# First stage: later thirds' token tiles normalised and transposed during the preceding third, kept in DRAM, loaded into the operand buffers block by block

## The chip, the cores and the metric

The kernel runs on one core of one Trainium2 chip. The metric is the device time of one execution in microseconds, the median of several runs. Nothing is changed in what is computed.

## The reference

One layer of a hybrid encoder over 16 learned meta tokens and 2048 input tokens (together T = 2064), width 1024, float32:

```
p  = rms_norm(h, norm_mix_pre) @ w_in                  # 1024 -> 3080 columns
oa = rg_lru_group(p[:, :512])                          # columns "a": convolution, gates, linear recurrence
ob = forgetting_attention_group(p[:, 512:2056])        # "q", "k", "v" and 8 gate columns "f"
oc = rwkv7_group(p[:, 2056:])                          # columns "c": delta-rule recurrence over time
h  = h + rms_norm(concat(oa, ob, oc) @ w_out, norm_mix_post)
f  = causal_dwconv3(rms_norm(h, norm_ffn_pre) @ ffn_up)
h  = h + rms_norm((gelu(gate) * val) @ ffn_down, norm_ffn_post)
```

The change is within the first line: the norm of h, and the product with w_in.

## The kernel before

**Stages.** In order: the first stage (input projection, with the two recurrences beside it), attention, output projection with the second norm, FFN up, FFN down. Everything between stages goes through scratch tensors in DRAM (scr).

**The first stage.** The product is made transposed: 128 columns of w_in are the stationary operand, up to 400 tokens the moving one, and the contraction of 1024 is KD = 8 slices of 128. For precision every operand is split into a rounded part and a remainder (hi, lo: xh, xl for the tokens, wh, wl for the weights), and a product is three matmuls (mm3, lines 174 to 176; tile psp). The tokens are cut in three parts, each of two blocks (w_in_tokens, L182): 400 and 384 tokens, 384 and 384, 256 and 256. The operands of a part's two blocks stand in pool xn, which has one buffer for each of xh0, xl0, xh1, xl1.

**The norm.** w_in_norm (L189) makes a part's operands, tile by tile of 128 tokens: norm_transpose (L123) loads the tile into a buffer xt (tag nt_x), takes the sum of squares on ScalarE (L119), the inverse root in nine short steps on VectorE (L86 to L95), scales (L132), and transpose_split (L136) turns it with eight transposes on TensorE (L145, tile pst) in two groups; each group is rounded into xh by ScalarE (L151) and the remainder written to xl by VectorE (L152). Parts 1 and 2 are normalised when the part before has been issued, since only then the xn buffers come free. In part 1 all tiles but the first two are held until the last weight of part 0 has been rounded (issue_after).

**The units.** w_in_part (L304) goes through 24 units of 128 columns in the order c (8), a (4), k, v, q (4 each). A unit takes its weights once (w_in_weights, L211) and runs both blocks; the last two units run together, both on block 0 and then both on block 1. In part 0 the weights are loaded raw (nt_x), rounded (L168, L169) and written to scr wk; parts 1 and 2 load both halves from there (L222), into pool w (two buffers each of wh and wl) or, for half of part 2's units, into nt_x. Ahead of the units, w_in_gate (L275) makes the eight gate columns for both blocks, two matmuls a slice (L293, L294; tile psf), from a weight fw in pool w. Results leave PSUM by turns through ScalarE (L57, L240) and VectorE (L59, L241) into pool st, and SP stores them (L242, L243, L249, L268).

**Pools.** nt has four nt_x buffers (raw weights, xt, the splitting of w_out, some weights), st two of each tag, the PSUM pool of the stage five banks for psp, psf, pst.

**What runs beside.** recurrences (L2070) is a list of small steps: the gate's cumulative sum, and for nine blocks of 256 tokens the RWKV block (tiles named rw.., PSUM rps and eps, lines 1015 to 1359) and the LRU block (L1426 to L1468, tile rwlraw its load). Beside.advance hands out 1.25 steps after each step of a unit, from the 13th unit of part 0 on; what is left over when the units are done is issued then (L2183), and runs on into the attention. In parts 1 and 2 two more helpers are called between units: up_sums (loads us, L1681, sums on GpSimd) and, in part 1, w_out_split.

**Order.** Nearly all DMAs are issued from SP, in one in-order queue. The program issues instructions in the order told here; the build then draws up each engine's order by priority along a simulated timeline, and issue_after is an order by hand on one engine. The engines run in the order drawn up.

## Time and profile before

| | |
|---|---|
| time, median of 3 runs | 2990.34 us (2987.96 to 2994.16) |
| span of the profiled execution (the page has no other time of it) | 2994.3 us |
| first stage, from the first psp to the last | 42 to 880 us |
| PE, DVE, ACT busy over the span | 97%, 68%, 49% |
| mean granted TensorE clock | 0.976 |

In the profile PE is the matmul side of TensorE and PEld its weight load, DVE is VectorE, ACT ScalarE, POOL GpSimd, SP the engine that issues the DMAs. A row of the busy time by stretch gives for each engine its busy time and, in brackets, its instructions, then the granted clock, the busy share of the 16 DMA engines and their rate. A row of the timeline gives start, duration, engine, line, operation and tile, and in square brackets the idle time ahead of it with what ended it. Durations of matmuls include their way through the array, so successive ones overlap: their rate is read from their starts.

### The profile page before, as it was taken

What the parts mean: (1) busy time and instruction counts of PE and PEld (TensorE: products, weight loads), DVE (VectorE), ACT (ScalarE), POOL (GpSimd) and SP (SyncE); (2) the same over time, 40 slices, a digit from 0 to 9 for tenths busy, and PEclk for the clock granted to TensorE, in tenths of its full rate; (3) what the DMA queues carried; (4) which work ended last, traced back from release to release, by engine and by line L of the source; (5) the groups of instructions that cost most, each with busy time, mean ns of one, the idle gap of its engine ahead of it and who ended that gap; (6) DMA issues with size and microseconds to landing.
All of it is one profiled execution on the core that took longest, in us unless ns stands there. A gap on an engine that the chain in (4) does not pass through costs nothing.

```text
span 2994.3 us, 52802 instructions
## 1 busy us (share of the span) xinstructions
PE 2898.0 (97%) x18694; PEld 2486.3 (83%) x18694; DVE 2037.0 (68%) x3937; ACT 1480.8 (49%) x2858; POOL 1319.7 (44%) x1567
## 2 busy tenths in 40 slices
PE   6999999999999999999999999999999999999998
PEld 6998899888886655665568999999999999787887
DVE  5258644765677776565636998898778787656766
ACT  4246332443346554455634656666565665424333
POOL 1002122121223665666843667446655544656443
PEclk9999899999988999999999999999999999999999
DMA  6777469676644347544336565577777764436453
GB/s 210 239 235 226 135 230 310 203 242 194 199 129 101 95 109 208 134 113 109 77 96 212 183 198 179 173 220 211 208 208 218 222 198 128 158 116 220 145 174 120
DMA packets 469190, 530.49 MB, mean 177 GB/s; under 512 B 85710, under 2 KB 355736, under 8 KB 467372
## 3 DMA queue, kind: packets, MB, share of 16 engines
q1 hardware_dynamic: 468156, 526.17, 58.2%
q8 instruction: 147, 2.41, 0.3%
q0 software_dynamic: 768, 0.93, 0.1%
q14 instruction: 119, 0.97, 0.1%
HBM read 368.07 MB, written 158.90 MB: 176 GB/s over the span
## 4 chain that ended last, share of the span: by engine, by line
PE 59%; DVE 4%; POOL 2%; DMA 2%; ACT 2%; issue 2%; SPq 0%; DVEq 0%; POOLq 0%; ACTq 0%
PE psu L174 9%; PE psu L175 9%; PE psu L176 9%; PE po L716 4%; PE psd L174 4%; PE psd L175 4%; PE psd L176 4%; PE mx L566 2%; PE pswo L174 2%; PE pswo L176 2%; PE pswo L175 2%; PE sc L693 2%; PE sc L694 2%; POOL acc L737 1%; DVE mc L571 1%
## 5 line engine op out<-in xcount | busy, mean ns | idle before, releaser
L175 PE MATMUL psu<-xo,uw 128*128 128x344 f32 x1848 | 591.4, 320 | 0.0
L174 PE MATMUL psu<-xo,uw 128*128 128x344 f32 x1848 | 586.0, 322 | 2.7 <-ACT u L1828 1.2
L176 PE MATMUL psu<-xo,uw 128*128 128x344 f32 x1848 | 581.9, 320 | 1.3 <-POOL uw L1657 1.0
L174 PE MATMUL psp<-xh,wh 128*128 128x384 f32 (+2 forms) x1152 | 380.8, 331 | 0.0
L176 PE MATMUL psp<-xh,wl 128*128 128x384 f32 (+2 forms) x1152 | 378.0, 328 | 0.0
L175 PE MATMUL psp<-xl,wh 128*128 128x384 f32 (+2 forms) x1152 | 377.8, 328 | 0.0
L1657 DVE TENSOR_TENSOR uw<-uq,uw 128x512 fp32r<-128x512 f32 x341 | 320.3, 944 | 59.2 <-ACT uw L1656 56.7
L174 PEld LDWEIGHTS psu<-xo,uw 128*128 128x128 f32 x1848 | 345.8, 188 | 4.3 <-DVE vb L1848 1.8
L176 PEld LDWEIGHTS psu<-xo,uw 128*128 128x128 f32 x1848 | 345.7, 188 | 2.1 <-POOL uw L1657 1.3
L175 PEld LDWEIGHTS psu<-xo,uw 128*128 128x128 f32 x1848 | 347.1, 188 | 0.0
L1656 ACT ACTIVATE uw<-uq 128x512 fp32r<-128x512 f32 x462 | 287.9, 627 | 95.7 <-PE psu L176 44.4
L698 ACT ACTIVATE p<-sc,bias 128x512 f32<-128x512 f32 (+4 forms) x352 | 197.9, 590 | 142.3 <-PE sc L694 119.2
L571 DVE TENSOR_REDUCE mc<-mx 128x1 f32<-128x512 f32 (+6 forms) x352 | 190.0, 565 | 113.6 <-PE mx L566 80.1
L1796 DVE SCALAR_TENSOR_TENSOR uy<-psu,ffn_cols,uy 128x342 f32<-128x342 f32 (+1 forms) x390 | 220.4, 567 | 61.4 <-ACT uy L1794 59.7
L1804 POOL TENSOR_TENSOR uy<-uy,uy 128x342 f32<-128x342 f32 (+1 forms) x132 | 146.5, 1110 | 229.2 <-DVE uy L1796 55.9
L737 POOL TENSOR_TENSOR acc<-acc,p 128x512 f32<-128x512 f32 (+3 forms) x208 | 222.7, 1073 | 48.4 <-DVE acc L737 23.4
L1657 POOL TENSOR_TENSOR uw<-uq,uw 128x512 fp32r<-128x512 f32 x121 | 184.4, 1524 | 133.8 <-ACT uw L1656 116.0
L174 PEld LDWEIGHTS psp<-xh,wh 128*128 128x128 f32 x1152 | 220.1, 191 | 8.7 <-issue 7.3
L176 PEld LDWEIGHTS psp<-xh,wl 128*128 128x128 f32 x1152 | 220.1, 191 | 7.0 <-issue 5.1
L175 PEld LDWEIGHTS psp<-xl,wh 128*128 128x128 f32 x1152 | 220.1, 191 | 5.0 <-issue 3.2
L1657 DVE TENSOR_TENSOR fo<-u,fo 128x896 fp32r<-128x896 f32 x88 | 101.6, 1155 | 133.7 <-ACT fo L1656 133.2
L1656 ACT ACTIVATE fo<-u 128x896 fp32r<-128x896 f32 x88 | 81.2, 923 | 206.6 <-PE psd L176 118.1
(488 smaller groups left out, 6409.4 us busy)
## 6 DMA issues: line engine op xcount, KB each, us to landing
uq<-scr_us SPq DMA_DIRECT2D x220, 256.0 KB
uq<-in_ffn_up_dram SPq DMA_DIRECT2D x209, 256.0 KB
wl<-scr_wk SPq DMA_DIRECT2D x48, 512.0 KB
wh<-scr_wk SPq DMA_DIRECT2D x48, 512.0 KB
u<-scr_ff SPq DMA_DIRECT2D x88, 256.0 KB
scr_ff<-uy SPq DMA_DIRECT2D x110, 171.0 KB
raw<-in_w_in_dram SPq DMA_DIRECT2D x24, 512.0 KB
scr_wk<-wh SPq DMA_DIRECT2D x24, 512.0 KB
```

The costliest lines, as they stand in the source:

```text
L174: nc.tensor.matmul(out, ah, bh, start=first, stop=False, skip_group_check=more)
L175: nc.tensor.matmul(out, ah, bl, start=False, stop=False, skip_group_check=more)
L176: nc.tensor.matmul(out, al, bh, start=False, stop=last, skip_group_check=more)
L566: nc.tensor.matmul(ps[:rows, : e - a], q3[:, qo : qo + rows], k2[:, a:e], start=True, stop=not last)
L571: self.reduced = nc.vector.tensor_reduce(mc[:rows, i, ci : ci + 1], ps[:rows, : e - a], axis=AX.X, op=ALU.max)
L698: last = nc.scalar.activation(p[:rows, :w], ps[:rows, :w], AF.Exp, bias=bias[:rows, j : j + 1])
L716: mm = nc.tensor.matmul(po[at : at + 64, c0:n], v1[:rows, j], p[:rows, : n - c0], start=start and i < 2, stop=end and i + 2 >= len(group), ...
L737: eng.tensor_tensor(a, ps_[0][0][:rows, c0:n] if start and i == 1 else a, p[:rows, : n - c0], op=ALU.add)
L1656: core.nc.scalar.activation(hi, src, AF.Copy)
L1657: (eng or core.nc.vector).tensor_tensor(lo, src, hi, op=ALU.subtract)
L1796: core.conved = stt(y[:, :n], src[:, i : n + i], cw[:, 44 * i + cc : 44 * i + cc + 1], y[:, :n], op0=ALU.mult, op1=ALU.add)
L1804: core.pooled = nc.gpsimd.tensor_tensor(v[:, :n], g[:, :n], v[:, :n], op=ALU.mult)
```

## The change

The norm of parts 1 and 2 is taken apart. w_in_ahead makes the tiles of a later part while the part before runs: six tiles of part 1 after the units 0, 2, 4, 6, 8, 10 (counted from 0) of part 0, four tiles of part 2 after the units 2, 6, 10, 14 of part 1. Load, squares, root and scaling are as before (normed); the transposed groups are copied from PSUM once, unsplit (by turns ScalarE and VectorE), and stored to a new scratch tensor xt. At the start of part 1 and of part 2 w_in_fetch loads each block in four pieces of two slices into the buffer of the remainder, rounds each on ScalarE and takes the remainder in place on VectorE. The hold of part 1's tiles is gone. In parts 1 and 2 the gate and the first two units go block by block (gate, unit 0, unit 1 on block 0, then the same on block 1), and the gate's weights and unit 0's stand in nt_x.

```diff
--- before.py
+++ after.py
@@ -120,17 +120,21 @@
     return rstd_from(core.nc, v, ss, width, core.apart)
 
 
-def norm_transpose(core, pools, psum, src, rows, gain, pieces, after=nullcontext):
+def normed(core, pools, src, rows, gain):
 
     nc = core.nc
     xt = pools["nt"].tile([P, D], F32, tag="nt_x", name=core.n("xt"))
     nc.sync.dma_start(xt[:rows], src)
     junk = pools["st"].tile([P, D], BF16, tag="stv", name=core.n("xj"))
     v = pools["nt"].tile([P, 6], F32, tag="rs", name=core.n("rs"))
-    with after():
-        rs = rstd_of(core, v[:rows], xt[:rows], D, junk[:rows])
+    rs = rstd_of(core, v[:rows], xt[:rows], D, junk[:rows])
     nc.vector.scalar_tensor_tensor(xt[:rows], xt[:rows], rs, gain[:rows], op0=ALU.mult, op1=ALU.mult)
-    transpose_split(core, psum, xt, rows, pieces)
+    return xt
+
+
+def norm_transpose(core, pools, psum, src, rows, gain, pieces):
+
+    transpose_split(core, psum, normed(core, pools, src, rows, gain), rows, pieces)
 
 
 def transpose_split(core, psum, xt, rows, pieces):
@@ -186,7 +190,7 @@
     return [tiles[a:e] for a, e in zip(cuts, cuts[1:])]
 
 
-def w_in_norm(core, pools, psum, x, meta, gain, part):
+def w_in_blocks(core, pools, part):
     blocks = []
     for b, tl in enumerate(w_in_tokens(part)):
         t0 = tl[0][0]
@@ -194,28 +198,63 @@
         hi = pools["xn"].tile([P, KD, n], F32R, tag=f"xh{b}", name=core.n("xh"))
         lo = pools["xn"].tile([P, KD, n], F32R, tag=f"xl{b}", name=core.n("xl"))
         blocks.append((t0, n, tl, hi, lo))
+    return blocks
+
+
+def w_in_norm(core, pools, psum, x, meta, gain):
+    blocks = w_in_blocks(core, pools, 0)
     for t0, n, tl, hi, lo in blocks:
         for s, rows in tl:
             src = meta if s < META else x[s - META : s - META + rows, :]
-            late = part == 1 and (s, rows) not in blocks[0][2][:2]
-            after = (lambda: core.tc.issue_after(core.rounded.ins)) if late else nullcontext
-            norm_transpose(core, pools, psum, src, rows, gain, [(hi, lo, s - t0, 0, rows)], after)
+            norm_transpose(core, pools, psum, src, rows, gain, [(hi, lo, s - t0, 0, rows)])
     return blocks
 
 
+def w_in_ahead(core, pools, psum, x, gain, scr, part):
+
+
+    nc = core.nc
+    for b, tl in enumerate(w_in_tokens(part)):
+        for s, rows in tl:
+            xt = normed(core, pools, x[s - META : s - META + rows, :], rows, gain)
+            for k0 in range(0, KD, 4):
+                ps = psum.tile([P, 4, P], F32, tag="mm", name=core.n("pst"))
+                for k in range(4):
+                    nc.tensor.transpose(ps[:, k], xt[:, (k0 + k) * P : (k0 + k + 1) * P], core.ident[:])
+                o = pools["st"].tile([P, 4, P], F32, tag="stv", name=core.n("xs"))
+                core.evac(o[:], ps[:])
+                c = s - tl[0][0]
+                nc.sync.dma_start(scr["xt"][part - 1, b, :, k0 : k0 + 4, c : c + P], o[:])
+            yield
+
+
+def w_in_fetch(core, pools, scr, part):
+    nc = core.nc
+    blocks = w_in_blocks(core, pools, part)
+    for b, (t0, n, tl, hi, lo) in enumerate(blocks):
+        for k0 in range(0, KD, 2):
+            ks = slice(k0, k0 + 2)
+            raw = lo[:, ks].bitcast(F32)
+            nc.sync.dma_start(raw, scr["xt"][part - 1, b, :, ks, :n])
+            nc.scalar.activation(hi[:, ks], raw, AF.Copy)
+            nc.vector.tensor_tensor(lo[:, ks], raw, hi[:, ks], op=ALU.subtract)
+    return blocks
+
+
 def w_in_kept(scr, c0):
 
     return scr["wk"][c0 // P]
 
 
-def w_in_weights(core, pools, w_in, c0, scr, part):
+def w_in_weights(core, pools, w_in, c0, scr, part, first=False):
 
     if part == 0:
         src = w_in[:, c0 : c0 + P].rearrange("(k p) c -> p k c", p=P)
         pair = split_load(core, pools["w"], (pools["nt"], "nt_x", None), src, [P, KD, P], "w")
     else:
-        core.turns += part == 2
-        pl, tags = (pools["nt"], ("nt_x", "nt_x")) if core.turns % 4 > 1 else (pools["w"], ("wh", "wl"))
+        core.turns += part == 2 and not first
+        other = first or core.turns % 4 > 1
+        pl, tags = (pools["nt"], ("nt_x", "nt_x")) if other else (pools["w"], ("wh", "wl"))
         pair = [pl.tile([P, KD, P], F32R, tag=tag, name=core.n(s)) for s, tag in zip(("wh", "wl"), tags)]
     for t, kept in zip(pair, w_in_kept(scr, c0)):
         t = t[:].rearrange("p k c -> p (k c)").bitcast(F32)
@@ -276,7 +315,8 @@
 
     nc = core.nc
     c0 = 2048
-    w = pools["w"].tile([P, KD, P], F32R, tag="wh", name=core.n("fw"))
+    pl, tag = (pools["nt"], "nt_x") if part else (pools["w"], "wh")
+    w = pl.tile([P, KD, P], F32R, tag=tag, name=core.n("fw"))
     flat, kept = w[:].rearrange("p k c -> p (k c)").bitcast(F32), w_in_kept(scr, 3 * D)[0]
     if part == 0:
         raw = pools["st"].tile([P, KD, 8], F32, tag="stv", name=core.n("fraw"))
@@ -297,12 +337,11 @@
         o = pools["st"].tile([8, 400], F32, tag="stl", name=core.n("fo"))
         nc.vector.tensor_tensor(o[:, :n], ps[0:8, :n], a[:, :n], op=ALU.add)
         nc.sync.dma_start(scr["f"][:, t0 : t0 + n], o[:, :n])
-    yield False
-    yield True
+        yield
 
 
 def w_in_part(core, pools, psum, w_in, blocks, scr, part):
-    yield from w_in_gate(core, pools, psum, w_in, blocks, scr, part)
+    gate = w_in_gate(core, pools, psum, w_in, blocks, scr, part)
     units = [("c", 2056 + P * i) for i in range(8)] + [("a", P * i) for i in range(4)]
     units += [(s, c + P * i) for s, c in (("k", 1024), ("v", 1536), ("q", 512)) for i in range(4)]
     waiting = [None]
@@ -314,7 +353,20 @@
             waiting[0]()
         waiting[0] = after
 
-    for kind, c0 in units[:-2]:
+    first = 2 if part else 0
+    some = [
+        (w_in_weights(core, pools, w_in, c0, scr, part, i == 0), kind, c0) for i, (kind, c0) in enumerate(units[:first])
+    ]
+    for block in blocks:
+        next(gate)
+        yield part == 0 and block is blocks[-1]
+        for w, kind, c0 in some:
+            step(w, block, kind, c0)
+            yield block is blocks[-1]
+    if part:
+        yield True
+
+    for kind, c0 in units[first:-2]:
         w = w_in_weights(core, pools, w_in, c0, scr, part)
         for block in blocks:
             step(w, block, kind, c0)
@@ -343,6 +395,7 @@
         "part": dr.tile([SEQ, D], F32, name="scr_part"),
         "us": dr.tile([NFF, P, 4 * 512], F32, name="scr_us"),
         "wo": dr.tile([KD, 2, P, D], F32, name="scr_wo"),
+        "xt": dr.tile([2, 2, P, KD, 384], F32, name="scr_xt"),
         "wk": dr.tile([3 * D // P + 1, 2, P, D], F32, name="scr_wk"),
         "ds": dr.tile([DOWN_PAIRS, P, 4 * 512], F32, name="scr_ds"),
     }
@@ -2028,6 +2081,8 @@
 
 
 READY = 13
+
+AHEAD = range(1, 13, 2), range(4, 18, 4)
 PACE = 1.25
 
 WIDE = (0, 5)
@@ -2132,18 +2187,20 @@
             pools = {"xn": pool(p1a, "xn", 1), "nt": pool(p1a, "nt", 4), "w": pool(p1a, "w", 2), "st": pool(p1a, "st", 2)}
             sums = up_sums(core, pool(p1a, "us", 1), a["ffn_up"], scr, EARLY)
             split_out = w_out_split(core, pools["nt"], a["w_out"], scr)
-            following = w_in_norm(core, pools, ps_mm, x, meta, g_pre, 0)
+            ahead = [w_in_ahead(core, pools, ps_mm, x, g_pre, scr, part) for part in (1, 2)]
             for part in range(3):
-                blocks = following
+                blocks = w_in_fetch(core, pools, scr, part) if part else w_in_norm(core, pools, ps_mm, x, meta, g_pre)
                 if part == 0:
                     zeros = pools["st"].tile([P, PAD], F32, tag="sth", name="zeros")
                     nc.vector.memset(zeros[:], 0.0)
                     for r in range(0, A_ROWS + C_ROWS, P):
                         nc.gpsimd.dma_start(scr["p"][r : r + P, 0:PAD], zeros[:])
                 units = w_in_part(core, pools, ps_mm, a["w_in"], blocks, scr, part)
-                for _ in range(READY if part == 0 else 0):
+                for i in range(READY if part == 0 else 0):
                     while not next(units):
                         pass
+                    if i in AHEAD[0]:
+                        next(ahead[0])
                 if part == 0:
                     attn_consts(core)
                     rk = rwkv_consts(
@@ -2173,13 +2230,13 @@
                         continue
                     if part == 1 and i > 1:
                         next(split_out, None)
+                    if part == 1 and i in AHEAD[1]:
+                        next(ahead[1])
                     if part and i % 2 == 0:
                         with tc.issue_after(core.loaded.ins):
                             next(sums, None)
                     i += 1
                 run(sums) if part == 2 else None
-                if part < 2:
-                    following = w_in_norm(core, pools, ps_mm, x, meta, g_pre, part + 1)
         beside.finish()
         for _ in R.ending:
             pass
```

## The prediction

> **What bounds the kernel now.** I read the page first (engines, clock), then busy time by stretch, then the order of TensorE's work (PE) at the two places where one third of the first stage ends and the next begins.
>
> ```profile
> span 2994.3 us, 52802 instructions
> ...
> PE 2898.0 (97%) x18694; PEld 2486.3 (83%) x18694; DVE 2037.0 (68%) x3937; ACT 1480.8 (49%) x2858; POOL 1319.7 (44%) x1567
> ...
> PEclk9999899999988999999999999999999999999999
> ```
>
> PE is busy for 97% of the span, so only PE time that is wasted can be won: waits, or work at a reduced granted clock. The stretches of the first stage and the one behind it:
>
> ```profile
> core 0: us, PE busy (x) PEld busy (x) DVE busy (x) ACT busy (x) POOL busy (x), PEclk, DMA share, GB/s
> 42.00:150.00 108.00, 108.00 (x605) 108.00 (x604) 30.66 (x42) 31.93 (x44) 0.40 (x1) 1.00 0.70 230
> 150.00:279.00 129.00, 128.28 (x736) 118.04 (x736) 89.70 (x220) 65.38 (x128) 9.82 (x18) 1.00 0.73 233
> 279.00:323.00 44.00, 38.87 (x390) 32.43 (x389) 39.23 (x104) 27.34 (x54) 13.40 (x20) 0.69 0.37 114
> 323.00:617.00 294.00, 291.95 (x2420) 267.12 (x2419) 159.33 (x387) 99.53 (x187) 57.30 (x84) 0.98 0.71 232
> 617.00:627.00 10.00, 7.98 (x54) 7.11 (x53) 7.63 (x17) 6.00 (x13) 2.97 (x4) 0.86 0.94 306
> 627.00:880.00 253.00, 246.58 (x2622) 224.41 (x2622) 162.90 (x415) 108.75 (x223) 56.64 (x91) 0.97 0.62 190
> 880.00:1120.00 240.00, 221.62 (x1964) 150.37 (x1961) 182.70 (x502) 134.37 (x291) 130.80 (x205) 0.87 0.46 107
> ```
>
> Parts 0, 1 and 2 are rows 1 and 2, row 4 and row 6. Between them lie two seams of 44 and 10 us. In the first the granted clock is 0.69 and DVE is busy 39.2 of 44 us. The timeline of PE shows its edges:
>
> ```profile
> 278.74 0.34 PE L176 MATMUL psp<-xh,wl 128*128 128x384 f32 x1
> 278.91 1.80 PE L145 MATMUL pst<-ident,xt 128*128 128x128 f32 x15
> ...
> 320.21 0.34 PE L294 MATMUL psf<-xl,fw 128*128 128x384 f32 x1
> ...
> 322.68 0.34 PE L294 MATMUL psf<-xl,fw 128*128 128x384 f32 x1
> 322.86 0.34 PE L174 MATMUL psp<-xh,wh 128*128 128x384 f32 x1
> ```
>
> The products of the projection (psp) stop at 279 and resume at 323. From 320.21 to 322.68 there are 14 steps: 0.176 us per 384-wide matmul at full clock.
>
> **What the change removes at seam 1.** The other work that PE does there (recurrences rps and eps, gate psf) remains. Busy time in the two seams by tile, columns PE, PEld, DVE, ACT; first rps, then eps, then psf:
>
> ```profile
> 279.00:323.00 44.00, 17.78 (x296) 16.03 (x296) 4.89 (x9) 5.12 (x10) 0.69 0.37 114
> ```
> ```profile
> 279.00:323.00 44.00, 6.01 (x12) 2.68 (x12) 0.88 (x2) 2.71 (x6) 0.69 0.37 114
> ```
> ```profile
> 279.00:323.00 44.00, 8.09 (x32) 7.01 (x32) 0.54 (x1) 0.48 (x1) 0.69 0.37 114
> 617.00:627.00 10.00, 3.44 (x17) 3.15 (x17) 0.00 (x0) 0.21 (x1) 0.86 0.94 306
> ```
>
> At full clock rps and eps need about (17.8 + 6.0) × 0.69 = 16.4 us, psf 32 × 0.176 = 5.6: 22 of the 44 us. The other **22.0 us** go if the operands are there on time. Where part 0 has psp without a break, row 1 above, the clock is 1.00, so the recurrences should keep full clock between products.
>
> **Seam 2.** The same timeline:
>
> ```profile
> 617.25 3.62 PE L145 MATMUL pst<-ident,xt 128*128 128x128 f32 x28
> 622.88 0.66 PE L145 MATMUL pst<-ident,xt 128*128 128x128 f32 x4 [2.00 <-DVE xl L152]
> ...
> 629.26 0.28 PE L294 MATMUL psf<-xl,fw 128*128 128x256 f32 x1
> ...
> 631.06 0.28 PE L174 MATMUL psp<-xh,wh 128*128 128x256 f32 x1
> ```
>
> A 256-wide matmul takes 1.80 / 15 = 0.12 us. The 10 us hold 17 psf and 5 psp, 2.6 us at that rate; **7.4 us** go.
>
> **What comes back elsewhere.** The transposes stay PE work. A transpose takes 3.62 / 28 = 0.129 us; six tiles of eight are 48 × 0.129 = **6.2 us**, now in part 0, and four tiles are 32 × 0.129 = **4.1 us** in part 1. PE has no free time there (108.0 of 108), so both count in full. Net: seam 1 −15.8, seam 2 −3.3, together **−19.1 us**.
>
> The rest of each tile, grouped by line in seam 1 (ahead of the bar: busy us, mean ns behind it):
>
> ```profile
> L152 DVE TENSOR_TENSOR xl<-pst,xh 128x512 fp32r<-128x512 f32 x12 | 7.9, 679 | 0.3 <-ACT xh L151 0.3
> L151 ACT ACTIVATE xh<-pst 128x512 fp32r<-128x512 f32 x12 | 6.8, 612 | 0.4 <-PE pst L145 0.3
> L132 DVE SCALAR_TENSOR_TENSOR xt<-xt,rs,g_pre 128x1024 f32<-128x1024 f32 x2 | 2.5, 1272 | 0.0
> L119 ACT ACTIVATE xj<-xt 128x1024 bf16<-128x1024 f32 x2 | 2.2, 1102 | 0.2 <-DMA xt<-in_x_dram 0.2
> ```
>
> A tile made ahead costs ACT 1.1 + one evacuation 0.6, DVE 1.3 + nine short root steps + one evacuation 0.7: for six tiles some 10 us of ACT and 20 of DVE, about 12 beside the root steps. In part 0 up to 150 us DVE is busy 31 of 108 and ACT 32, so this lies beside products. It would surface if it made the weights late; they have slack:
>
> ```profile
> L168 ACT ACTIVATE wh<-raw 128x1024 fp32r<-128x1024 f32 x13 | 13.8, 1059 | 33.1 <-PE psp L175 32.0 <-DMA raw<-in_w_in_dram 1.1
> ```
>
> In 42:150 the rounding of a weight waits 32.0 us for the buffer that PE still reads and 1.1 for its transfer, so a raw buffer (nt_x, four) lent to a tile is not missed. SP's queue gets one load and two stores per tile where there was one load, and eight loads per fetch. The added traffic is ten 0.5 MB stores and as much in loads back, 10.5 MB: 45 us at row 4's 232 GB/s, in 600 us of a share near 0.7. This stretch bore more (tile psp: PE, clock, DMA share, GB/s):
>
> ```profile
> 500.00:520.00 20.00, 18.06 (x100) 1.00 0.97 353
> ```
>
> Psp held 18 of 20 us at 353 GB/s. But part 1's third and fourth tile come near there. I take **+2 us** for transfers that come late, with weights of part 2's third unit, which now wait for the gate's nt_x buffer; bounds 0 and 7 (one pair of 512 KB weights late by its whole transfer, priced below). The gate's weights and the first unit's, moved to nt_x, cost nothing: they can now load before the last products end. Gate and two units by block hold the same matmuls as before.
>
> **What the new wait costs.** A block's buffers come free with the last product that reads them. The last two units of a part run block by block, so block 0 is free 48 × 0.176 = 8.4 us ahead of the part's end. Its fetch is 1.57 MB in seam 1, 1.05 MB in seam 2. The nearest transfers, from the queue's and ACT's timelines:
>
> ```profile
> 284.70 1.15 SPq L127 DMA_DIRECT2D xt<-in_x_dram x2
> ...
> 287.60 23.57 SPq L1426 DMA_DIRECT2D rwlraw<-scr_p x3
> ```
> ```profile
> 291.77 1.06 ACT L119 ACTIVATE xj<-xt 128x1024 bf16<-128x1024 f32 x1 [0.25 <-DMA xt<-in_x_dram]
> ```
>
> Two loads, 1.05 MB, took 7 us from first issue to use; 1.57 MB then some 9 us. Splitting a piece of 128x768 is scaled from these 896-wide rows of the page:
>
> ```profile
> L1657 DVE TENSOR_TENSOR fo<-u,fo 128x896 fp32r<-128x896 f32 x88 | 101.6, 1155 | 133.7 <-ACT fo L1656 133.2
> L1656 ACT ACTIVATE fo<-u 128x896 fp32r<-128x896 f32 x88 | 81.2, 923 | 206.6 <-PE psd L176 118.1
> ```
>
> ACT 0.8, DVE 1.0 us. Behind the last piece that is 1.8 us alone, some 6 behind DVE's other work (70% busy in row 2). Block 0 is ready 11 to 15 us after its release, 2 to 7 after the part's end: I take **+5 us**, nearer the upper end since DVE is fullest there. Block 1 has the gate and two units on block 0 to hide behind (16 + 48 matmuls, 11.2 us, and the recurrences): 0. In seam 2: ready 8 to 11 us against 8.4, and block 1 against 64 × 0.12 = 7.7 us of cover: **+2**, bounds 0 and 6. While the fetch waits, SP's later stores and loads stand behind it: outputs in two-buffer st tiles, then the PSUM banks, then PE itself; that is the slow rival below.
>
> A rule on the clock: the Trainium skill, "TensorE: Matmul & The Clock Gate", Part 1, says that the clock falls to half after one idle window of about 3.4 us, and Part 4 that transposes do not count as activity. The trace agrees: 0.69 and 0.86 in the seams, where transposes and small products ran. By it my 5 us wait would leave another window at half clock, an estimate of 1.7 us more, and the sum would be −8. A rule on transfers: the Trainium skill, "DMA: Bandwidth & Descriptors", Anatomy of one DMA, gives 2.0 us + bytes / 436 GB/s (measured on GpSimd's path), an estimate of 5.6 us for 1.57 MB; the sum would then be about −13. The measured 7 us for 1.05 MB decides, and no run here shows the 436.
>
> **The sum.** −19.1 + 5 + 2 + 2 = **−10 us**. It is made against the profiled execution: the page gives its span, 2994.3, and nothing around it; that is 0.1 us over the longest of the three times and 4.0 over their median of 2990.3. Carried to the median: **2980**. The build draws up each engine's order from a simulated timeline, so orders far from the seams can shift; I allow ±8 us.
>
> **Rivals.**
> *The fetch is wholly hidden.* DVE loses about 20 us of norm work in seam 1 and gets 8 × 1.0 back, so block 0 is on time: −19 us, 2971. For it: DVE's 39 of 44. Against: DVE is 70% busy before the seam as well.
>
> *The queue holds the fetch back (slower).* SP issues in order. From 287.6 it spent 23.6 us on three issues, with waits. If block 0's loads stand behind such a wait at seam 1, PE has only recurrences at half clock, as now: −10 + 23.6 = +14, 3004. From 16 us of such waiting on it is slower by over 0.2% (about 6 us, what a measurement of this kernel can tell from no change). For it: the row. Against: that wait fell where DVE was filled by the norms, which leave.
>
> *The recurrences give it back.* They run on into the attention:
>
> ```profile
> 880.00:900.00 20.00, 18.71 (x178) 13.83 (x175) 14.72 (x39) 1.93 (x6) 8.23 (x6) 0.50 0.69 163
> ```
>
> In 880:1120 the clock is 0.87 and PE 222 of 240. In the seam they caught up by 16 us of PE work. If their chain, not PE, ends that stretch, products that end 10 us earlier lengthen it by as much: 2988 to 2990. For it: the clock of 0.50 at 880. Against: they are handed out by units, and PE's order stays theirs.
>
> **How the numbers follow.** Forecast 2980: 0.42. Hidden, 2971: 0.20. Given back, 2989: 0.14. Queue, 3004: 0.24. Faster: 0.62, same 0.14, slower 0.24. The range runs from 2963 (hidden, with the 8 us of shifted order) to 3003, which takes in all but the queue's worse half and the outermost shifts. The forecast's own range, by its bounds of 0 to 7, 0 to 6 and 0 to 7: −19 to +1, 2971 to 2991.
>
> **What would show it.** Right: no transposes of xt left between the parts; psp breaks off for some 5 us plus gate at seam 1 and 2 at seam 2; granted clock there above 0.9; part 0 longer by 6 us, part 1 by 4; DVE's share in the seam down. Wrong: gate products waiting on DVE or on the fetch for over 15 us, SP standing ahead of the fetch, psp in part 0 waiting for weights, or 880:1120 longer by what the seams lost.

## The result and the profile after

The changed kernel takes 3015.5 us (median of four executions; 3006.2 to 3018.5) where the kernel before, measured beside it, takes 2992.3: a ratio of 1.0074, 95% interval 1.0054 to 1.0094. It is slower by 0.7%; the forecast was 2980 and the range ended at 3003. Executions of one and the same kernel scatter by 5 to 29 us, the longer ones mostly with the lower mean granted clock (here 3006.2 us at 0.979, 3018.5 at 0.971). So verdicts below go by ratios of several executions, and stages, each read from one execution, are trusted where several kernels show them alike.

The page of the changed kernel:

```profile
span 3016.2 us, 52920 instructions
...
PE 2895.6 (96%) x18694; PEld 2486.8 (82%) x18694; DVE 2048.8 (68%) x3943; ACT 1491.2 (49%) x2864; POOL 1315.9 (44%) x1567
...
PEclk9999999999987899999999999999999999999999
...
DMA packets 483078, 540.98 MB, mean 179 GB/s; under 512 B 86286, under 2 KB 368600, under 8 KB 481260
```

TensorE (PE) is busy for 2.4 us less than before (2898.0) in a span that is 21.9 us longer: what was added is time in which PE does nothing. To find the place, busy time by stretch, cut at the first and the last product (psp) of each part; the last two rows are the **tail**, from the last psp until 30% of the attention's po products are done:

```profile
core 0: us, PE busy (x) PEld busy (x) DVE busy (x) ACT busy (x) POOL busy (x), PEclk, DMA share, GB/s
43.67:284.20 240.53, 240.53 (x1386) 230.27 (x1386) 132.71 (x283) 104.65 (x184) 10.27 (x19) 1.00 0.80 256
284.20:288.06 3.86, 3.86 (x27) 3.82 (x26) 3.78 (x8) 2.76 (x6) 0.00 (x0) 1.00 1.01 270
288.06:623.28 335.22, 321.77 (x2784) 292.21 (x2784) 193.40 (x482) 127.55 (x237) 66.98 (x104) 0.96 0.69 227
623.28:627.92 4.64, 4.64 (x34) 4.01 (x34) 3.56 (x6) 1.31 (x3) 0.87 (x1) 1.00 1.07 373
627.92:891.45 263.53, 254.41 (x2687) 230.20 (x2685) 163.23 (x412) 109.80 (x223) 60.95 (x97) 0.96 0.61 187
891.45:977.25 85.80, 70.15 (x599) 50.60 (x598) 63.15 (x172) 44.73 (x99) 31.43 (x52) 0.72 0.52 118
977.25:1165.76 188.51, 166.30 (x1355) 107.72 (x1355) 135.72 (x367) 98.14 (x208) 102.36 (x161) 0.91 0.43 103
```

The same cuts of before, those that the prediction does not show:

```profile
42.15:278.74 236.59, 235.87 (x1338) 225.66 (x1338) 120.11 (x261) 97.05 (x172) 10.23 (x19) 1.00 0.72 232
...
626.72:877.96 251.24, 244.82 (x2612) 222.87 (x2612) 161.62 (x413) 108.57 (x222) 56.64 (x91) 0.98 0.62 191
877.96:964.33 86.37, 78.56 (x678) 57.35 (x677) 66.44 (x192) 44.11 (x98) 34.24 (x54) 0.71 0.54 122
964.33:1147.36 183.03, 168.50 (x1381) 107.60 (x1381) 134.26 (x359) 98.68 (x210) 103.83 (x162) 0.93 0.44 104
```

Seam 1 shrank from 44.1 to 3.9 us, with PE never idle; seam 2 from 9.6 to 4.6. Against these 45 us stand part 0 (+3.9), part 1 (294.2 to 335.2, +41.0), part 2 (+12.3) and the tail (+4.9): together 17 of the 22 us, the rest in small pieces outside these cuts. The recurrence steps that the seam had held had to reappear in part 1. The question is what the rest is.

### The profile page after: what moved, and what is told of

The parts are those of the page before. It is cut to its first block, busy times and chain, and to the rows that moved or that the text cites. A ratio compares the mean times of both kernels' runs of the same rounds, so it can differ in the third digit from the quotient of the medians.

```text
span 3016.2 us, 52920 instructions
## 1 busy us (share of the span) xinstructions
PE 2895.6 (96%) x18694; PEld 2486.8 (82%) x18694; DVE 2048.8 (68%) x3943; ACT 1491.2 (49%) x2864; POOL 1315.9 (44%) x1567
## 4 chain that ended last, share of the span: by engine, by line
PE 79%; DVE 7%; DMA 5%; POOL 3%; ACT 3%; issue 2%; SPq 1%; DVEq 0%; POOLq 0%; ACTq 0%
PE psu L178 9%; PE psu L179 9%; PE psu L180 9%; PE psp L180 5%; PE psp L178 5%; PE psp L179 5%; PE psd L178 4%; PE psd L179 4%; PE psd L180 4%; PE po L769 4%; PE mx L619 2%; PE pswo L178 2%; PE pswo L179 2%; PE pswo L180 2%; PE sc L746 2%
## 5 line engine op out<-in xcount | busy, mean ns | idle before, releaser
L624 DVE TENSOR_REDUCE mc<-mx 128x1 f32<-128x512 f32 (+5 forms) x352 | 190.0, 565 | 122.2 <-PE mx L619 83.3
L178 PEld LDWEIGHTS psp<-xh,wh 128*128 128x128 f32 x1152 | 221.9, 193 | 10.2 <-issue 7.3
```

What stands on the lines that cost most here:

```text
L178: nc.tensor.matmul(out, ah, bh, start=first, stop=False, skip_group_check=more)
L624: self.reduced = nc.vector.tensor_reduce(mc[:rows, i, ci : ci + 1], ps[:rows, : e - a], axis=AX.X, op=ALU.max)
```

## The experiments

Three theories stood first: **A**, the recurrences cost more between products than in the seam; **B**, one accident of order; **C**, late transfers and tiles. After these **T** (the tiles made ahead in part 1 lose), **F** (the fetch and the weights at the start of part 2 lose) and **O** (any change draws up another order of the small steps, and that costs). The other letters (T1, T2, P, S, W) are explained in the expectation that first uses them. The **projection** is the time from the first psp to the last, seams included. In the diffs `NEW` names the parts that fetch; with `(1, 2)` it is the changed kernel, with `()` the kernel before.

**1. Without recurrences**, in the kernel before and in the changed one (one run each):

```diff
-    for b in ((0, 1, 2), (3, 4, 5), (6, 7, 8))[part]:
+    for b in ():
```

> The kernel before without the RWKV and LRU blocks beside the projection (the gate's cumulative sum stays; the rows of scr mix that they would write are zeroed). Leaves out: both recurrences. It is the base for e1_norec_after: the first stage should shrink well below 880 us, seam 1 keep its stop of products. Theory A (the recurrences used the seam, and cost more among the products) expects seam 1 here to be 44 - 24 = some 20 us, nearly all of it norm work. Theory C (the added traffic or the fetch itself costs) says nothing on this one.

> The changed kernel without the RWKV and LRU blocks (rows of scr mix zeroed). Leaves out: both recurrences. Theory A: with no recurrences to hand back, the change must gain what it takes from the seams less the transposes: the last product of part 2 comes 10 to 20 us earlier than in e1_norec_before. Theory C (traffic, fetch, weights that come late): it gains nothing or loses 10 us or more, as in the full kernel. Theory B (one wait of 7 us in part 1 and the half clock behind it, an accident of the order) expects a gain of 10 or more here too, since that wait is one of the recurrence.

Measured: 2698.3 and 2717.5 us. These are single executions, and 19 us is within what two of one kernel can differ by; the stages say more. The projection is 16.7 us longer with the change (610.1 to 626.8), though seam 1 shrinks by 22.6: it is part 1 that grows, by 32.9. Part 1 without recurrences, before and changed:

```profile
280.04:492.48 212.44, 211.13 (x1202) 208.16 (x1201) 44.73 (x101) 39.87 (x67) 34.13 (x44) 1.00 0.87 290
```
```profile
262.89:508.23 245.34, 222.44 (x1249) 219.81 (x1249) 58.77 (x112) 47.19 (x78) 39.09 (x48) 0.96 0.84 284
```

A expected a gain of 10 to 20 us with no recurrence in the program, so A falls. Much of the cost can be seen here, in the waits of PE in part 1 of the changed kernel without recurrences (waited for: us in total, times, longest):

```profile
PE pst L223 <- DVE xt L131: 18.8, 4, 10.4
```

Each of the four tiles made ahead in part 1 makes PE wait for its scaling. The fourth of them, by the timelines of the DMA queue, ACT, DVE and PE:

```profile
412.64 0.60 SPq L1557 DMA_DIRECT2D scr_wo<-wo  x1
413.30 0.48 SPq L127 DMA_DIRECT2D xt<-in_x_dram  x1
```
```profile
422.20 1.06 ACT L119 ACTIVATE xj<-xt 128x1024 bf16<-128x1024 f32 x1 [5.52 <-DMA xt<-in_x_dram]
```
```profile
425.17 1.28 DVE L131 SCALAR_TENSOR_TENSOR xt<-xt,rs,g_pre 128x1024 f32<-128x1024 f32 x1
```
```profile
426.51 1.75 PE L223 MATMUL pst<-ident,xt 128*128 128x128 f32 x7 [10.36 <-DVE xt L131]
```

The load goes out behind the transfers of w_out's pieces, which share its buffers (nt_x); it takes 8.9 us from issue to first use (the four loads took 6.4 to 8.9), where seam 1 of the kernel before had two loads in 7; the root and the scaling follow, and the transposes stand in PE's order ahead of the next unit's products, so PE waits 10.4 us. In part 0 of the full changed kernel a load at 60.4 us fed transposes at 91.0, and nothing waited; here 13 us lie between issue and transposes. B falls as the whole, with no recurrence there to meet an accident; C is nearest.

**2. One part alone**: `NEW = (1,)` and `NEW = (2,)`.

> The change at part 1 alone: six tiles ahead in part 0, fetch at the start of part 1; part 2 normalised between the parts as before, no tiles ahead in part 1. Theory A (seam 1's recurrence work comes back dearer): slower than before by 8 to 20 us. Theory B (the 7 us wait stands behind the fourth tile ahead in part 1): that wait is gone, time -5 to +5 us against before. Theory C (traffic): about half of the loss, +10 us.

> The change at part 2 alone: four tiles ahead in part 1, fetch at the start of part 2; seam 1 as before, with its held tiles. Theory A: seam 2 holds hardly any recurrence work, so -7.4 + 4.1 = -3 us, within 5 us of before. Theory B (tiles ahead in part 1 push the recurrence's short chain on VectorE behind them): slower by 8 to 15 us. Theory C: about half of the loss, +10 us.

Measured: part 1 alone 2979.8 us, ratio 0.9953 (0.9934 to 0.9973), **faster**; part 2 alone 3023.7, ratio 1.0092 (1.0059 to 1.0126), slower. None of the three theories had either time. The first half of the change gains; the loss is in the half that serves part 2. Seam 1, part 1 of the first kernel, then part 1 of the second:

```profile
282.01:285.87 3.86, 3.86 (x27) 3.82 (x26) 3.25 (x8) 3.28 (x7) 0.00 (x0) 1.00 1.00 299
285.87:600.94 315.07, 310.93 (x2736) 280.49 (x2736) 185.25 (x455) 119.75 (x225) 68.26 (x104) 0.99 0.69 226
```
```profile
319.75:629.26 309.51, 298.64 (x2468) 273.06 (x2468) 166.18 (x417) 107.25 (x201) 54.76 (x84) 0.98 0.72 233
```

With the change at part 1 alone, part 1 is 20.9 us longer than before: the recurrences that left the seam, and 2.8 us (16 × 0.176) of the gate's products, those on block 1. The four tiles make it 20.1 longer again (335.2 against 315.1), or 15.3 where seam 1 was left as it was (309.5 against 294.2). Of the 20.1, PE is idle for 9.3; of the 10.8 that it is busy, the transposes are 4.1 by the prediction's price, and the granted clock is 0.96 instead of 0.99.

**3. The half that serves part 2, taken apart.** Made in part 1 and stored but never read (only); made in part 0 (part0); normalised two units ahead of the transposes (early); the whole change with all tiles made in part 0 (all0).

```diff
 only, NEW = ():       if part == 1 and i in AHEAD[1]: next(ahead[1])
 part0, NEW = (2,):    if i in (4, 6, 8, 10): next(ahead[1])      # in part 0, none in part 1
 early, NEW = (2,):    if part == 1 and (i in AHEAD[1] or i + 2 in AHEAD[1]): next(ahead[1])
                       # and in w_in_ahead, behind normed(...):  if part == 2: yield
 all0, NEW = (1, 2):   as part0
```

> The kernel before, with the four tiles of part 2 also normalised, transposed and stored during part 1 (places 4, 8, 12, 16) but never read: part 2 normalises its own as before. The output is the same; the work is doubled. Theory T (the loss is made by the tiles ahead in part 1): part 1 ends about 12 us later than before, as where the change was made at part 2 alone, and the whole is 12 to 20 us slower, 3005 to 3013. Theory F (the loss is made by the fetch and by weights that are held up at the start of part 2): only the 4 us of transposes, 2995 to 3000, and no wait of over 3 us in part 1.

> The change at part 2 alone, but its four tiles are made in part 0 (places 4, 6, 8, 10), where one of part 1's six tiles cost 0.9 to 1.1 us; part 2 fetches as in the change. Theory T: part 1 is as before, part 2 starts 3 us earlier than before by seam 2, the whole is 2985 to 2992. Theory F: part 1 as before, but part 2's first four units still lose 8 to 13 us against before, the whole is 3000 to 3010.

> The change at part 2 alone, each tile's load and normalisation two units ahead of its transposes (places 2, 6, 10, 14 for the first, 4, 8, 12, 16 for the second). Theory T1 (the transposes come late because the x load is issued late, and hold the products behind them): no wait of PE at the transposes, part 1 ends at most 5 us later than before, the whole 3000 to 3010 against 3024 with load and transposes at one place. Theory T2 (the loss in part 1 is the added traffic at 0.98 of the DMA engines, wherever the load is issued): 3018 to 3028.

> The whole change, but part 2's four tiles are made in part 0 as well (places 4, 6, 8, 10 beside part 1's 1, 3, 5, 7, 9, 11). If the two seams add up: by theory T the gain of part 1's seam (-14) and -5 to 0, 2972 to 2982; by theory F -14 and +8 to +15, 2985 to 2995.

| kernel | us | ratio to before (95%) | part 1 against before | seam 2 | part 2 |
|---|---|---|---|---|---|
| only | 3021.7 | 1.0082 (1.0058 to 1.0106) | +13.7 | 8.6 | +9.5 |
| part0 | 3007.9 | 1.0037 (1.0021 to 1.0054) | +0.2 | 2.1 | +9.3 |
| early | 3030.4 | 1.0103 (1.0071 to 1.0135) | +13.1 | 2.1 | +36.7 |
| all0 | 3000.2 | 1.0014 (1.0002 to 1.0026) | −1.4 (part 0 +24.1) | 2.1 | +1.0 |

In part 1 the first kernel does what T said: tiles that nobody reads cost 13.7 us there. Its whole time is 9 us above T's range. F falls as the whole of it, since part 2 is 9.5 us longer there without any fetch. Part 1 of only, then of early:

```profile
318.99:626.93 307.94, 297.70 (x2455) 273.26 (x2454) 170.60 (x447) 108.98 (x205) 55.19 (x84) 0.97 0.72 233
```
```profile
320.90:628.19 307.29, 299.98 (x2456) 275.65 (x2456) 167.93 (x405) 106.28 (x199) 54.88 (x84) 0.97 0.72 235
```

Made in part 0, the tiles cost part 1 nothing, and seam 2 gains 7.6 us; yet that kernel is slower. T did not allow this; F did, in time (3000 to 3010) and in part 2 (a loss of 8 to 13). But the same fetch loses only 1.0 us in part 2 of all0, so the fetch alone is not what lengthens part 2. Seam 2, part 2 and tail of part0:

```profile
613.81:615.88 2.07, 2.07 (x18) 2.07 (x18) 2.07 (x5) 0.49 (x1) 0.00 (x0) 1.00 0.70 168
615.88:876.41 260.53, 251.88 (x2570) 229.18 (x2569) 160.03 (x411) 110.13 (x225) 61.88 (x96) 0.93 0.62 190
876.41:968.23 91.82, 82.71 (x709) 61.76 (x708) 70.87 (x192) 46.54 (x102) 32.02 (x53) 0.72 0.49 113
968.23:1157.41 189.18, 168.64 (x1394) 109.31 (x1394) 140.57 (x376) 99.02 (x211) 102.70 (x162) 0.92 0.42 102
```

Part 2 gives back 9.3 us with fewer PE instructions (2570 against 2612), and the tail, which has the 44 others, 11.6. The early kernel shows what an earlier load does. In the changed kernel the fourth tile of part 1 stood so (PE, ahead of the products of unit 16):

```profile
495.61 1.03 PE L1120 MATMUL eps<-rwsq,gat 128*4 128x256 f32 x4 [1.10 <-ACT rwe L1111]
503.77 2.07 PE L1139 MATMUL eps<-rwix,spr 4*128 4x256 f32 x4 [7.14 <-DVE rwix L79]
505.77 1.97 PE L223 MATMUL pst<-ident,xt 128*128 128x128 f32 x8
507.39 0.67 PE L178 MATMUL psp<-xh,wh 128*128 128x384 f32 x1
507.86 0.52 PE L179 MATMUL psp<-xl,wh 128*128 128x384 f32 x1
...
510.42 0.36 PE L178 MATMUL psp<-xh,wh 128*128 128x384 f32 x1
```
```profile
489.84 0.50 SPq L127 DMA_DIRECT2D xt<-in_x_dram  x1
```
```profile
503.82 1.28 DVE L131 SCALAR_TENSOR_TENSOR xt<-xt,rs,g_pre 128x1024 f32<-128x1024 f32 x1
```

The wait is put down to rwix, a chain of short DVE steps between two recurrence products (gat and spr). But the tile was scaled only at 505.1, and the products of the next unit stand behind its transposes, so nothing was there to fill PE meanwhile. The load is not what made this tile late: ScalarE took its squares without waiting for a transfer,

```profile
497.47 1.04 ACT L119 ACTIVATE xj<-xt 128x1024 bf16<-128x1024 f32 x1
```

and VectorE, busy without a gap from 496.7 to 505.1, did the root in between the steps of rwix. The other three tiles of this part 1 were scaled 0.3 to 5.9 us ahead of their transposes and made PE wait nowhere. Nor is the wait an accident of one order: it is 7.0 to 7.2 us in the changed kernel at all four paces of experiment 5, in part 2 alone and in only, 5.4 in places3, and absent where only a half of a tile or none is made at these places, and in early. Where products stand between them, the same two products are further apart and nobody waits. The kernel before, and the early kernel, whose transposes come ahead of gat:

```profile
509.74 1.03 PE L1067 MATMUL eps<-rwsq,gat 128*4 128x256 f32 x4
...
523.36 1.13 PE L1086 MATMUL eps<-rwix,spr 4*128 4x256 f32 x4
```
```profile
509.15 1.03 PE L228 MATMUL pst<-ident,xt 128*128 128x128 f32 x8
510.12 1.03 PE L1129 MATMUL eps<-rwsq,gat 128*4 128x256 f32 x4
...
522.32 1.12 PE L1148 MATMUL eps<-rwix,spr 4*128 4x256 f32 x4
```

So the early load takes this wait away, as T1 said; the four tiles are now scaled 23 us and more ahead of their transposes. It does not take the loss away: part 1 is still 13.1 us longer than before, where T1 allowed an end 5 us later and load and transposes at one place cost 15.3. PE's longest wait in that part 1 is now 3.5 us for a weight,

```profile
PE psp L179 <- DMA wh<-scr_wk: 3.5, 1, 3.5
```

and part 2 is 36.7 us longer, with 4.4 us more of idle PE and a granted clock of 0.89 where before had 0.98; the cause was not followed up:

```profile
630.28:918.25 287.97, 277.18 (x2705) 248.07 (x2703) 165.27 (x419) 111.71 (x226) 63.39 (x98) 0.89 0.56 174
```

T1's time (3000 to 3010) failed by 20 us: a late tile is one cause, but not the sum of it. T2, that the traffic costs wherever the load is issued, fits part 1 better; its time (3018 to 3028) was passed by 2, and the same loads without transposes cost only 4.4 us there (loads, in 4).

The fourth kernel met neither theory's range. The recurrence steps of seam 1 stand in its part 0, not in part 1. Its projection takes 814.0 us, 21.8 less than before; its tail takes 291.0, 21.6 more, with a wait of 11.2 us in it:

```profile
PE mx L626 <- DMA k<-scr_cl: 11.2, 1, 11.2
```

**4. The tile's halves, and the order alone.** Only transposes and evacuations of a constant (ghost); only load, normalisation and store (loads); nothing but another pace of the recurrences in the kernel before (pace); the whole change with part 2's tiles one unit earlier (places3).

```diff
 ghost, NEW = ():     core.nc.tensor.transpose(ps[:, k], core.ident[:], core.ident[:])   # no load, no store
 loads, NEW = ():     core.evac(o[:].rearrange("p k c -> p (k c)"), xt[:, k0 * P : (k0 + 4) * P])   # no transposes
 pace:    -PACE = 1.25
          +PACE = 1.26
 places3: -AHEAD = range(1, 13, 2), range(4, 18, 4)
          +AHEAD = range(1, 13, 2), range(3, 17, 4)
```

> The kernel before, and at places 4, 8, 12 and 16 of part 1 eight transposes of the unit matrix with two evacuations into a buffer that nobody reads: TensorE's and the evacuations' share of a tile made ahead, with nothing to wait for. Theory P (the tiles ahead lose because transposes that come late hold the products behind them): about the 4 us of the transposes, 2994 to 3000. Theory O (any insertion here makes the build draw up another order of small recurrence steps, and that order costs 10 to 20 us): 3005 to 3015, with the 7 us wait of the spr product at about 500 us.

> The kernel before, and at the same places load, normalisation and store of a tile, without its transposes (the scaled rows are copied and stored as they are, and never read): the transfers' and DVE's and ACT's share. Theory P: 2990 to 2998, since nothing stands in TensorE's queue. A theory of traffic (4 MB more at 0.9 to 1.0 of the DMA engines): 3000 to 3012 with TensorE waiting for weights. Theory O: anything from 2985 to 3015.

> The kernel before with the same work throughout; only the pace at which recurrence steps are handed out beside the products is 1.26 a step instead of 1.25, so that the orders of all engines are drawn up anew. Theory P: within 5 us of before. Theory O: it moves by 10 us or more, to either side.

> The whole change with part 2's tiles one unit earlier in part 1 (places 3, 7, 11, 15 instead of 4, 8, 12, 16). Theory P: the late loads are as late, 3010 to 3018. Theory O: another order, and the 17 us between units 14 and 16 go or move; 2990 to 3020.

Measured: ghost 3011.8 us, ratio 1.0055 (1.0033 to 1.0078); loads 3005.2, 1.0039 (1.0025 to 1.0054); pace 3015.0, **1.0070** (1.0046 to 1.0093); places3 3041.4, 1.0156 (1.0124 to 1.0188). Part 1 of ghost and of loads:

```profile
322.70:623.51 300.81, 296.32 (x2452) 271.82 (x2452) 160.40 (x387) 101.87 (x191) 55.79 (x84) 0.98 0.69 227
```
```profile
323.26:621.85 298.59, 294.60 (x2420) 268.65 (x2420) 167.44 (x427) 106.56 (x199) 58.28 (x84) 0.98 0.74 243
```

Transposes with nothing to wait for cost 6.6 us there, transfers and scaling without transposes 4.4; the whole tiles of only, which must land first, 13.7. If the parts may be added, the lateness that comes with joining them is the 2.7 us that are left; and these are small numbers, since part 1 of the kernel before takes 290 to 296 us at the paces tried below. P's times for both were too low. O's time for ghost came out, but its 7 us wait is absent, so that wait belongs to the tile; the traffic theory's time for loads came out too, without its sign, as no product in parts 1 and 2 waits for a weight there. (The profiled executions of ghost and of only lie 8 and 10 us under the medians of their runs, that of loads 7 above; stages are read from the former, verdicts from the latter.) Places one unit earlier are 25 us worse than the change as made, outside both ranges; that was not followed up. The unexpected one is pace: the same work, one per cent more of it handed out at each step, costs as much as the whole change. Where, the tail shows:

```profile
875.21:949.10 73.89, 59.80 (x472) 42.16 (x472) 53.25 (x145) 33.72 (x75) 27.73 (x41) 0.82 0.62 134
949.10:1162.23 213.13, 185.50 (x1605) 123.06 (x1605) 155.44 (x413) 109.97 (x237) 110.20 (x174) 0.87 0.40 93
```

287.0 us against 269.4, with PE busy 245.3 against 247.1: 19 us more of idle PE; no other stage moved by more than 3. So a pair of kernels at one pace does not say what an edit costs. Both were taken at more paces.

**5. Both kernels at other paces, and part 1 alone at a second one**: `PACE` at 1.24, 1.20 (before), 1.26, 1.24, 1.20 (changed), 1.26 (`NEW = (1,)`).

> The kernel before with the recurrences handed out at 1.24 a step instead of 1.25. Theory O (the kernel before has a fortunate order, and any other costs it 10 to 20 us): 3005 to 3015. Theory S (what costs is recurrences that are handed out sooner; 1.26 was slower for that): 2985 to 2995, no slower than 1.25.

> The kernel before with the pace at 1.20. Theory O: 3000 to 3015. Theory S: the recurrences are later by 4%, and the tail behind the projection is longer by some 10 us: 2995 to 3010, with fewer recurrence steps in part 2.

> The whole change with the pace at 1.26. Theory O (the change's own work is a gain of some 10 us, hidden by the accident of the order): the three orders of the change scatter by 10 us and more, and at least one comes under the same pace of before: 2990 to 3010 here, under before's 3015 at 1.26. Theory W (the change's own work and waits cost 20 us): 3012 to 3025, within 8 us of the change at 1.25.

> The whole change with the pace at 1.24. Theory O: 2990 to 3010, under before at the same pace. Theory W: 3012 to 3025. Theory S (one more hand-out of recurrence steps in each later part of the changed kernel is what costs): 3000 to 3008, and lower still at a lower pace.

> The whole change with the pace at 1.20, where the kernel before takes 3001 us. Theory O: the difference from before at the same pace is again another number than at 1.25 (+22), 1.26 (+3) and 1.24 (+4); anything between -10 and +15, so 2991 to 3016. Theory W: +20, 3015 to 3027.

> The change at part 1 alone (2980 at 1.25, 14 under before) with the pace at 1.26, where the kernel before takes 3015. If the gain of the first seam is its own and not an accident of the order: 2995 to 3005 by the same 14 us. If it was an accident: 3010 or more.

Ratios to the kernel before at 1.25, with intervals; and from the profiled execution of each the projection (first psp to last, seams included) and the tail, in us:

| pace | before | its projection, tail | changed | its projection, tail |
|---|---|---|---|---|
| 1.20 | 1.0015 (1.0001 to 1.0029) | 833.0, 260.0 | 1.0047 (1.0027 to 1.0067) | 850.8, 265.7 |
| 1.24 | 1.0083 (1.0061 to 1.0105) | 831.6, 293.7 | 1.0100 (1.0077 to 1.0123) | 857.0, 269.9 |
| 1.25 | 1 | 835.8, 269.4 | 1.0074 (1.0054 to 1.0094) | 847.8, 274.3 |
| 1.26 | 1.0070 (1.0046 to 1.0093) | 834.0, 287.0 | 1.0084 (1.0062 to 1.0106) | 857.4, 275.1 |

The tail's worst row, of before at 1.24, beside its best, at 1.20:

```profile
945.83:1166.60 220.77, 189.35 (x1606) 125.24 (x1606) 152.76 (x411) 108.67 (x234) 106.94 (x172) 0.85 0.38 89
```
```profile
954.18:1134.14 179.96, 163.12 (x1377) 107.28 (x1377) 137.25 (x370) 97.90 (x209) 102.48 (x162) 0.94 0.44 104
```

Read down the projection's columns: before, it takes 832 to 836 us at every pace; changed, 848 to 857. The change costs 12 to 25 us there at each of four paces: that loss is its own, and W is right on this stage. (At 1.20 the profiled execution of before lies 11 us under its median and that of the changed kernel 8 above, so that row's difference may be too large.) The other kernels agree. The projection takes 848 to 877 us in all eight kernels with recurrences that make whole tiles in part 1, 842 and 843 with ghost's and loads' halves of them, and 814 to 837 in all eight that make none there.

The tails read otherwise: before 260 to 294, changed 266 to 275. Counted to the attention's last po product instead, it is 658 to 684 us against 664 to 667. O is right on the tail, where before at 1.25 is a good throw and at 1.24 and 1.26 a bad one (what a tail of 270 to 294 us waits on was not settled). In whole times neither theory holds throughout: W's ranges came out at 1.26 and 1.24 and O's at 1.20. S falls: before at 1.24 is slower, and its tail at 1.20 is 9 us shorter, not 10 longer. In the whole time the change costs 22 us at 1.25, 10 at 1.20, and 5 and 4 at 1.24 and 1.26, where the intervals overlap widely (differences of the ratios, times 2995 us; at 1.20 the intervals just touch). It was slower or not to be told apart, and faster at none.

The change at part 1 alone at 1.26 takes 2988.7, ratio 0.9983 (0.9970 to 0.9996), 26 us below before at that pace, a larger gain than either expectation had. It is faster at both paces, and at 1.25 it is the version that beats both kernels: 2979.8 us. But the gain does not come from one place: at 1.25 its projection is 11.1 us shorter than before's and its tail 10.2, at 1.26 the projection 2.4 and the tail 18.3, beside before's bad tail. Part 1 grows by 29.9 us there instead of 20.9. What the first half gains by itself is thus 2 to 11 us by these executions, and the rest may be the throw of the tail. Whether all tiles made in part 0, with a projection shorter still, would beat it under another pace was not tried.

## Why the prediction was wrong

From the forecast −10 us to the +22 of the two profiled executions are 32 us: part 1's tiles make 14 of them, part 2 12, the tail 5 and small pieces outside the cuts 5, less 4 that the seams and part 0 gave beyond the forecast.

- *Seam 1, "22.0 us go", net −15.8 with part 0's transposes:* right in kind, and in size at this pace. The seam is 3.9 us; 40.3 went, and 20.9 came back in part 1 (recurrences 18.1, the gate on block 1 2.8), so 19.4 went. With part 0's 5.1 in that kernel it is −14.3, and in the whole time −14 us, of which the tail's part may be luck. At 1.26 the same three stages gave −7.6.
- *"+5 us" for the first fetch:* too dear. PE is never idle in the 3.86 us between the products; the fetch is wholly hidden, as the first rival had it; that rival's total fell with the same step as the forecast's. The fetch took about what I had for it: the first of block 0's loads is issued at 274.1, ScalarE waits for one of the last two until 281.0, and the last remainder is done at 285.8, 11.7 us after the first issue, within the forecast 11 to 15. What I missed is the cover: the first issue is 10 us ahead of the part's last product, and the gate's products start at 285.2 on the slices that are done. The Trainium skill, "DMA: Bandwidth & Descriptors", Anatomy of one DMA, gave an estimate of 5.6 us for the fetch; the 6.9 us to that wait's end are longer. For one 0.5 MB load its rule gives an estimate of 3.2 us, and the slowest of the loads in part 1 without recurrences took 8.9 beside others.
- *Part 0 "+6.2":* 3.9 in the length of part 0; nothing there waits, as forecast.
- *Seam 2, "7.4 us go" and "+2" for its fetch:* 5.0 in the changed kernel, 7.6 with the tiles made in part 0. Right.
- *Part 1's tiles, 4.1 us of transposes and "+2 us for transfers that come late, bounds 0 and 7":* **the step that failed.** They cost 20.1 us. I had priced the tile by its PE time and by one pair of weights that comes late, and took part 0's cover for part 1's. In part 1 its transposes stand ahead of the next products in PE's order, so that a late tile stops the products themselves. Without recurrences, where the x load goes out behind w_out's transfers, this is 18.8 us in four waits. With them it is one visible wait of 7.1, where VectorE is late with a recurrence step and with the tile together, and 6.6 us at half clock behind it: the next products start 0.32 us apart for 3 us, then 0.18, and the spr products and the transposes ahead of them take 2.07 and 1.97 us where the rows of other kernels have 1.13 and 1.03, some 3 us lost in all. The Trainium skill, "TensorE: Matmul & The Clock Gate", Part 1, has the clock fall to half after one idle window of about 3.4 us and rise after as long a busy one; the rows agree that 7.1 us idle is enough, while the half rate lasts 6.6 us here. With the transposes' 4.1 that is some 14 of the 20.1. That the loss is made by tiles in part 1 is shown (20.1, 15.3 and 13.7 us in three pairs of kernels). **Why it is so much stays open in part**: with every tile scaled 23 us and more ahead (early) no such wait is left, and part 1 is still 13.1 us longer.
- *Part 2, no cost beyond the fetch:* wrong as well. It is 12.3 us longer. Some of this is recurrence work that came out of the tail (75 PE instructions more); the fetch is not needed for it (only: +9.5), and with the fetch and all tiles made in part 0 it is 9.3 in one kernel and 1.0 in the other. What lengthens it **stays open**.
- *"I allow ±8 us" for shifted orders:* too narrow. A pace of 1% gives +20 with no other edit. At 1.25 the before side was a good order, so the loss of the change showed undiminished; at 1.24 and 1.26 bad tails of before hide most of it.
- *The recurrences give it back:* not here, but in the kernel with part 2's tiles in part 0, where 7.6 us of seam became 20.9 of later part and tail, this is what the rows look like; that the chain of recurrences is the cause was not tried.
- *The queue holds the fetch back (the slow rival, 3004):* not seen at either seam: PE is idle in neither. The sign came out as it said, by another mechanism.

## What to carry to other kernels

Work moved beside a busy engine is free only if its inputs are there when its turn in that engine's order comes: look up, at the new place, what shares the moved load's buffers and queue, and what stands behind the moved instruction; one place's cover (part 0) is no evidence for another's (part 1). It may not be enough either: here tiles that were ready 23 us early still cost part 1 13 us. Where the build draws up the order, first alter something neutral, as the pace here, to learn how far the time moves without any cause, and compare stages over several such orders, not one pair of totals. Split a change that serves two places: at this pace one half gained 14 us and the other lost twice that.

## What the runs showed that was not expected

A change of 1% in the pace of the recurrences moves the kernel before by 0.70% and 0.83%, nearly all of it in one stretch of 270 us and mostly by idle time of PE. One x load of 512 KB took 8.9 us beside w_out's and the sums' transfers, more than two such loads took in the quiet seam (7). And PE ran at half its rate for 6.6 us behind an idle stretch of 7.1, so that the wait cost some 3 us besides.
